# A Strassen pair of the output projection behind both plain column groups

## The chip, the cores and the metric

The kernel runs on one core of one Trainium2 chip. The metric is the device time of one launch in microseconds (us), the median of several runs. All times of the profile are microseconds from the start of the profiled execution's span.

## The reference

One encoder layer: a norm, one input projection, two attention mixers of eight heads each, a gate, one output projection, a norm and the residual. Only the end matters here:

```python
y = jnp.einsum('blc,cd->bld', jnp.concatenate([ya, yb], axis=-1), w_out[layer])
h = h + rmsnorm(y, post_norm_g[layer])
return h[:, N_META:, :]
```

There are 512 real tokens, 2048 mixer channels (16 heads of 128) and 2048 output columns. `rmsnorm` scales a token's row by the inverse root of the mean square over all 2048 columns, so no output row can be finished before all its columns are there.

## The kernel before, in words

**Engines.** TensorE (PE) multiplies; its weight loads are listed as PEld. ScalarE (ACT) and VectorE (DVE) prepare operands and take results, GpSimd (POOL) does some elementwise work and issues the loads of one DMA queue, SyncE (SP) issues those of another. Each engine runs its instructions in the order in which they stand, so a waiting instruction holds up all behind it.

**Precision.** Every product is made of three: each operand is split into a high half (`wh`, `oh`; an ACT copy, L154 and L306) and a low half (`wl`, `ol`; a DVE subtraction, L155 and L309), and the three products without low times low are added up.

**Weights.** `w_out` comes in chunks of 128 x 1024 (512 KB). `todo` (L708) is the list of chunks in the order in which they are used; `fetch` (L194) hands out the next and keeps two more on the way: load on SP to `st`, split to `wh` and `wl`. Each of these tags has three buffers, so a split waits until PE is done with the chunk three before.

**The output projection.** The 2048 columns are four groups of 512, the 512 tokens four tiles of 128. Groups 0 and 3 are plain (`dense_out`, L767): 16 heads x 4 token tiles x 3 matmuls, 192 in all, with one chunk for two heads. Groups 1 and 2 are the middle pair, done by a Strassen scheme: token halves, head halves and the two groups make 2 x 2 blocks, and seven products (`product`, L860) stand for eight. Each product has four chunks of two heads and 48 matmuls. Three products use heads as they are (`of_y`), four use sums of heads:

- `first_sums` (L825) reads, for one of four head pairs, three half tiles `ts` back from DRAM scratch (`oscr`) on POOL's queue and makes from them the operands of the first two of these products (`u`, `v`), split into high and low: four DVE operations and two of ACT for each pair.
- `third_sum` (L834) and `fourth_sum` (L839) make the operands of the other two in the same buffers `u` and `v`, from loads on SP's queue.
- The weights of these four products and of one plain block product are sums of blocks of `w_out` held in `chain[0..3]` (shown as `ch`): two blocks are added while loading, by an accumulating DMA on POOL's queue; the later terms are added by DVE in `summed` (L691), one 128x1024 addition for each chunk, and one block is loaded afresh on the way (L696).

`C(r, x, u)` (L883) is where the results of the middle pair come together, in the output rows `y`: row tile 2x + u, column group 1 + r.

**Order before.** Plain group 0, the seven products, plain group 3. All four pairs' first sums are written out ahead of the first product, all third sums ahead of the fourth, all fourth sums ahead of the fifth; a scheduler then places the instructions on each engine. The last three chunks of group 3 are held together, so that each token tile ends alone and its row is finished (`finish`, L932) while PE works on the next: square sum (ACT), row scale `ry` (POOL), scaling and residual (DVE), store.

**Pools.** The buffers of this stage (`yp`) lie where the attention's lay and become free as attention ends. `pd` and `pd2` are the accumulator pools, four banks each.

## Time and profile before

| | us |
|---|---|
| runs, median (lowest to highest) | 965.67 (964.97 to 966.62) |
| the profiled execution, its own time | 966.93 |
| its span | 965.2 |
| PE busy in the span | 930.0 (96%) |
| DVE busy | 581.5 (60%) |
| ACT busy | 481.7 (50%) |
| POOL busy | 162.9 (17%) |
| last matmul of plain group 0 ends | 812.15 |
| last matmul of the program ends | 955.95 |

The page gives averages over a program whose stages have different limits: PE is busy 96% of the span, so the place to look is where it isn't. A row of the timeline reads: start, duration, engine, line, operation, output<-inputs, shapes, how many instructions are merged, and in brackets the idle time of the engine before it and what ended it. A row of the waits reads: who waited, for whom, the sum in us, how often, the longest.

### The profile page before, as it was taken

What the parts mean: (1) busy time and instruction counts of PE and PEld (TensorE: products, weight loads), DVE (VectorE), ACT (ScalarE), POOL (GpSimd) and SP (SyncE); (2) the same over time, 40 slices, a digit from 0 to 9 for tenths busy, and PEclk for the clock granted to TensorE, in tenths of its full rate; (3) what the DMA queues carried; (4) which work ended last, traced back from release to release, by engine and by line L of the source; (5) the groups of instructions that cost most, each with busy time, mean ns of one, the idle gap of its engine ahead of it and who ended that gap; (6) DMA issues with size and microseconds to landing.
All of it is one profiled execution on the core that took longest, in us unless ns stands there. A gap on an engine that the chain in (4) does not pass through costs nothing.

```text
span 965.2 us, 14195 instructions
## 1 busy us (share of the span) xinstructions
PE 930.0 (96%) x5498; PEld 812.2 (84%) x5498; DVE 581.5 (60%) x974; ACT 481.7 (50%) x844; POOL 162.9 (17%) x255
## 2 busy tenths in 40 slices
PE   9999999999999999999999999989999999796996
PEld 8899898989989898999997888877888888574884
DVE  6375676657476665748653183457555744698626
ACT  6664655546374554637552353354564734452421
POOL 0001010101010010101210042144122213210601
PEclk9999999999999999999999999999999999898998
DMA  9742122222322222222222232212122629976724
GB/s 331 259 157 93 66 87 87 88 87 77 98 77 93 70 99 76 79 86 78 87 78 88 88 91 84 73 59 65 56 77 77 190 95 307 277 224 227 266 82 175
DMA packets 39811, 117.16 MB, mean 121 GB/s; under 512 B 4640, under 2 KB 9632, under 8 KB 39616
## 3 DMA queue, kind: packets, MB, share of 16 engines
q1 hardware_dynamic: 36208, 104.71, 32.7%
q0 software_dynamic: 3392, 11.54, 4.0%
q8 instruction: 43, 0.70, 0.3%
q14 instruction: 24, 0.20, 0.1%
q10 hardware_dynamic: 144, 0.01, 0.0%
HBM read 107.85 MB, written 8.39 MB: 120 GB/s over the span
## 4 chain that ended last, share of the span: by engine, by line
PE 80%; DVE 7%; DMA 5%; POOL 3%; ACT 3%; issue 2%; SPq 0%; DVEq 0%; POOLq 0%; ACTq 0%
PE pd L63 54%; PE po L63 11%; PE sc L63 6%; PE pv L63 4%; PE tr L66 4%; DMA ts<-oscr 2%; DVE wl L155 2%; DVE qn L578 1%; POOL qn L592 1%; DMA ch<-in_w_o_dram 1%; POOL ssh L241 1%; DMA os<-oscr 1%; DVE ch L701 1%; DMA xs<-in_xT_dram 1%; ACT qn L650 0%
## 5 line engine op out<-in xcount | busy, mean ns | idle before, releaser
L63 PE MATMUL pd<-xh,wh 128*128 128x264 f32 (+1 forms) x992 | 333.2, 336 | 0.0
L63 PE MATMUL pd<-xh,wl 128*128 128x264 f32 (+1 forms) x992 | 325.0, 328 | 0.4 <-DVE wl L155 0.4
L63 PE MATMUL pd<-xl,wh 128*128 128x264 f32 (+1 forms) x992 | 324.8, 327 | 0.1
L154 ACT ACTIVATE wh<-st 128x1024 fp32r<-128x1024 f32 (+2 forms) x135 | 140.2, 1039 | 226.7 <-PE pd L63 91.0
L155 DVE TENSOR_TENSOR wl<-st,wh 128x1024 fp32r<-128x1024 f32 (+2 forms) x135 | 162.6, 1205 | 117.4 <-ACT wh L154 116.1
L63 PEld LDWEIGHTS pd<-xh,wl 128*128 128x128 f32 x992 | 186.6, 188 | 17.9 <-DVE wl L155 0.8
L63 PEld LDWEIGHTS pd<-xh,wh 128*128 128x128 f32 x992 | 187.3, 189 | 12.7 <-ACT wh L154 0.2
L63 PEld LDWEIGHTS pd<-xl,wh 128*128 128x128 f32 x992 | 187.5, 189 | 11.7 <-DVE xl L180 0.4
L63 PE MATMUL po<-wl,oh 128*128 128x512 f32 x176 | 70.5, 401 | 9.0 <-DVE wl L155 9.0
L63 PE MATMUL po<-wh,oh 128*128 128x512 f32 x176 | 71.2, 405 | 0.0
L63 PE MATMUL po<-wh,ol 128*128 128x512 f32 x176 | 70.3, 399 | 0.9 <-DVE ol L309 0.9
L463 ACT ACTIVATE p<-p,mx 128x528 f32<-128x528 f32 x64 | 46.5, 728 | 34.1 <-POOL mx L460 34.0
L453 DVE CUSTOM_DVE_ANT_0 p<-sc,dist 128x528 f32<-128x528 f32 x64 | 44.9, 701 | 24.0 <-PE sc L63 23.5
L309 DVE TENSOR_TENSOR pl<-tr,ph 128x512 fp32r<-128x512 f32 x64 | 43.3, 688 | 16.2 <-ACT ph L306 15.0
L306 ACT ACTIVATE ph<-tr 128x512 fp32r<-128x512 f32 x64 | 37.6, 590 | 30.8 <-PE tr L66 30.6
L63 PE MATMUL pd<-wh,xh 128*128 128x512 f32 x128 | 52.2, 408 | 0.8 <-DVE vf L300 0.8
L66 PE MATMUL tr<-ident,p 128*128 128x128 f32 (+1 forms) x320 | 50.7, 273 | 2.3 <-DVE gA L558 1.5
L63 PE MATMUL pd<-wh,xl 128*128 128x512 f32 x128 | 50.6, 395 | 0.0
L63 PE MATMUL pd<-wl,xh 128*128 128x512 f32 x128 | 50.5, 395 | 0.0
L66 PEld LDWEIGHTS tr<-ident,p 128*128 128x128 f32 (+1 forms) x320 | 37.2, 131 | 14.0 <-DVE gA L558 2.4
L63 PEld LDWEIGHTS po<-wl,oh 128*128 128x128 f32 x176 | 33.4, 190 | 18.2 <-DVE wl L155 10.3
L460 POOL TENSOR_SCALAR mx<-mx 128x2 f32<-128x2 f32 x32 | 12.1, 377 | 196.0 <-DVE mx L453 196.0
(204 smaller groups left out, 1565.3 us busy)
## 6 DMA issues: line engine op xcount, KB each, us to landing
st<-in_w_t_dram SPq DMA_DIRECT2D x82, 512.0 KB, 3.6
st<-in_w_o_dram SPq DMA_DIRECT2D x40, 512.0 KB, 4.2
st<-in_w_q_dram SPq DMA_DIRECT2D x16, 512.0 KB, 3.6
xs<-in_xT_dram SPq DMA_DIRECT2D x16, 264.0 KB, 5.4
xns<-in_xn_dram SPq DMA_DIRECT2D x8, 512.0 KB, 5.2
ch<-in_w_o_dram POOLq DMA_DIRECT2D x8, 512.0 KB, 7.5
xr<-in_xn_dram POOLq DMA_DIRECT2D x16, 256.0 KB, 6.1
os<-oscr SPq DMA_DIRECT2D x6, 512.0 KB, 3.7
```

The lines of the kernel that those rows point to most:

```text
L63: self._add(self.nc.tensor.matmul(out, lhsT, rhs, start=start, stop=stop), us)
L66: self._add(self.nc.tensor.transpose(out, in_, ident), 0.109)
L154: nc.scalar.activation(wh[:, c], st[:, c], AF.Copy)
L155: nc.vector.tensor_tensor(out=wl[:, c], in0=st[:, c], in1=wh[:, c].bitcast(F32), op=ALU.subtract)
L241: nc.gpsimd.tensor_tensor(out=dst, in0=dst, in1=mhalf[:rows, :dst.shape[1]], op=ALU.pow)
L306: nc.scalar.activation(dst, src, AF.Copy)
L309: nc.vector.tensor_tensor(out=dst, in0=src, in1=h.bitcast(F32), op=ALU.subtract)
L453: nc.vector.tensor_tensor_reduce(out=two(p), in0=sc[:, :, :HALF], in1=two(dist[:, w0:w0 + NT]), scale=1.0, scalar=-3.0e38, op0=ALU.add, op ...
L460: nc.gpsimd.tensor_scalar(out=mx, in0=mx, scalar1=-0.125, scalar2=1.0, op0=ALU.mult, op1=ALU.mult)
L463: nc.scalar.activation(p2[m], p2[m], AF.Exp, scale=0.125, bias=mx[:, m:m + 1], accum_out=sm[:, m:m + 1])
L578: nc.vector.scalar_tensor_tensor(out=raw[:, i, :], in0=raw[:, i, :], scalar=ss[:rows, i:i + 1], in1=g[:rows], op0=ALU.mult, op1=ALU.mult)
L592: nc.gpsimd.tensor_tensor(out=x, in0=x, in1=cos, op=ALU.mult)
```

## The change

Plain group 3 moves from behind the seven products to ahead of them, and the products stand last, with the accumulator pools exchanged. Beside the eight chunks of group 3 stand, chunk by chunk, the loads of the four chain tiles and the first sums, one pair to every second chunk. The third sums are written out step by step beside the fourth product, the fourth sums beside the sixth. `ts` has six buffers in place of five. The DVE additions to the chain lose their own priority. Row tiles 2 and 3 are finished while the last product runs. In that product the last three chunks are held together and run row tile by row tile; after each, `end` finishes row tile 0 or 1.

The diff, cut:

```diff
@@ todo
-    todo += whole(0) + plain(0, 0) + plain(0, 1) + summed((0, 0)) + summed((0, 1))
-    todo += summed((1, 0), fresh=(0, 0)) + summed() + plain(1, 1) + whole(3)
+    todo += whole(0) + whole(3) + plain(0, 0) + plain(0, 1) + summed((0, 0)) + summed((0, 1))
+    todo += summed((1, 0), fresh=(0, 0)) + summed() + plain(1, 1)
@@ summed
-                with tc.high_priority(rank[0]):
-                    nc.vector.tensor_tensor(out=chain[i], in0=chain[i], in1=st, op=ALU.add)
+                nc.vector.tensor_tensor(out=chain[i], in0=chain[i], in1=st, op=ALU.add)
@@ dense_out(g, pool, beside=None), after each chunk
+            if beside:
+                beside(j0 // 2)
@@ sums
-        t = yp.tile([P, 2, NP], F32, name="ts", tag="ts", bufs=5)
+        t = yp.tile([P, 2, NP], F32, name="ts", tag="ts", bufs=6)
...
-        nc.gpsimd.dma_start(out=chain[i], in_=block(1, 0, i))
...
-        nc.gpsimd.dma_start(out=chain[i], in_=block(1, 1, i), accum_op=ALU.add)
+    def first_chain(i):
+        nc.gpsimd.dma_start(out=chain[i], in_=block(1, 0, i))
+        nc.gpsimd.dma_start(out=chain[i], in_=block(1, 1, i), accum_op=ALU.add)
@@ product(ops, pool, beside=None, done=None)
+        for i in range(1 if done else 4):
+            ws = fetch()
             for u in range(2):
+                step(u, i, ws)
+            if beside:
+                beside(i)
+        if done:
+            last = [fetch(len(todo)) for _ in range(3)]
+            for u in range(2):
+                for i in range(3):
+                    step(u, 1 + i, last[i])
+                done(u, pss[u])
@@ order
+    def beside(s):
+        if s < 4:
+            first_chain(s)
+        if s % 2:
+            first_sums(s // 2)
+
     for t in range(TT):
         collect(0, t, first[t])
-    for i in range(4):
-        first_sums(i)
-    for u, ps in enumerate(product(of_y(0, 0), pd2)):
+    for t, ps in enumerate(dense_out(3, pd2, beside)):
+        collect(3, t, ps)
+    for u, ps in enumerate(product(of_y(0, 0), pd)):
...
-    for i in range(4):
-        third_sum(i)
-    for u, ps in enumerate(product(of_t(t2), pd)):
+    for u, ps in enumerate(product(of_t(t2), pd2, third_sum)):
...
-    for i in range(4):
-        fourth_sum(i)
-    for u, ps in enumerate(product(of_y(1, 1), pd2)):
+    for u, ps in enumerate(product(of_y(1, 1), pd)):
...
-    for u, ps in enumerate(product(of_t(t3), pd2)):
+    for u, ps in enumerate(product(of_t(t3), pd, fourth_sum)):
...
-    for u, ps in enumerate(product(of_t(t4), pd)):
-        TTv(out=C(1, 0, u), in0=C(1, 0, u), in1=ps, op=SUB)
-        block_done(1, 0, u)
@@ end
+    def row_block(t, r, x, g, far=False):
+        v = y[t][:, g * 512:(g + 1) * 512]
+        if far:
+            nc.scalar.activation(v, v, AF.Copy, scale=r)
+            TTp(out=v, in0=v, in1=x, op=ALU.add)
+        else:
+            nc.vector.scalar_tensor_tensor(out=v, in0=v, scalar=r, in1=x, op0=ALU.mult,
+                                           op1=ALU.add)
+        load(out[t * P:(t + 1) * P, g * 512:(g + 1) * 512], v)
...
+    with tc.high_priority(AHEAD):
+        for t in range(2):
+            r = row_scale(2 + t)
+            for g in range(4):
+                row_block(2 + t, r, xh_[t][g], g)
...
+    def end(u, ps):
+        TTv(out=C(1, 0, u), in0=C(1, 0, u), in1=ps, op=SUB)
+        square(u, 2, C(1, 0, u))
+        TTv(out=C(1, 0, u), in0=C(1, 0, u), in1=gpB[:, 1024:1536], op=ALU.mult)
+        if u == 1:
+            row_block(0, rs[0], xs(0, 1), 1)
+            row_block(0, rs[0], xs(0, 2), 2)
+        rs.append(row_scale(u))
+        row_block(u, rs[u], xs(u, 0), 0, True)
+        for g in ((3,) if u == 0 else (3, 1, 2)):
+            row_block(u, rs[u], xs(u, g), g)
+
+    product(of_t(t4), pd2, done=end)
-    dense_out(3, pd2, 6, finish)
```

Where the instructions stand then, on the engines that the order concerns. First DVE. Before, in the second product: the splits of that product's second, third and fourth chunk stand among the sums of pairs 1 and 2 (L829 and L831 make the sums out of `ts`, L309 their low halves).

```order
L155 TENSOR_TENSOR wl_8375<-st_8372,wh_8374 128x1024
L309 TENSOR_TENSOR ul1_8274<-ts_8265,uh1_8273 128x512
L831 TENSOR_TENSOR ts_8269<-ts_8269,ts_8265 128x512
L155 TENSOR_TENSOR wl_8397<-st_8394,wh_8396 128x1024
L309 TENSOR_TENSOR vl1_8279<-ts_8269,vh1_8278 128x512
L829 TENSOR_TENSOR ts_8282<-ts_8284,ts_8282 128x512
L831 TENSOR_TENSOR ts_8286<-ts_8286,ts_8282 128x512
L155 TENSOR_TENSOR wl_8415<-st_8412,wh_8414 128x1024
```

Now, in plain group 3: the splits of its sixth chunk (`wl_8363`) and seventh (`wl_8411`) with the sums of pairs 2 and 3 (L818, L820) and the first third sum (L829).

```order
L820 TENSOR_TENSOR ts_8472<-ts_8472,ts_8468 128x512
L309 TENSOR_TENSOR ul2_8476<-ts_8468,uh2_8475 128x512
L155 TENSOR_TENSOR wl_8363<-st_8360,wh_8362 128x1024
L309 TENSOR_TENSOR vl2_8481<-ts_8472,vh2_8480 128x512
L818 TENSOR_TENSOR ts_8544<-ts_8546,ts_8544 128x512
L820 TENSOR_TENSOR ts_8548<-ts_8548,ts_8544 128x512
L829 TENSOR_TENSOR ts_8835<-ts_8835,ts_8833 128x512
L309 TENSOR_TENSOR ul3_8552<-ts_8544,uh3_8551 128x512
L309 TENSOR_TENSOR vl3_8557<-ts_8548,vh3_8556 128x512
L155 TENSOR_TENSOR wl_8411<-st_8408,wh_8410 128x1024
```

The sums have moved from between chunks of 12 matmuls to between chunks of 24, and a split still stands behind a sum that waits for a load. Next POOL's DMA issues at the same place; before:

```order
L822 DMA ch2_8218<-in_w_o_dram 128x1024
L822 DMA ch3_8220<-in_w_o_dram 128x1024
L810 DMA ts_8248<-oscr0_78 128x2x256
L810 DMA ts_8250<-oscr0_78 128x2x256
L810 DMA ts_8252<-oscr4_82 128x2x256
L828 DMA ch0_8214<-in_w_o_dram 128x1024
L810 DMA ts_8265<-oscr1_79 128x2x256
L810 DMA ts_8267<-oscr1_79 128x2x256
```

Now (L824 loads a chain tile, L825 adds to it, L801 loads a `ts`):

```order
L825 DMA ch1_8215<-in_w_o_dram 128x1024
L801 DMA ts_8314<-oscr0_78 128x2x256
L801 DMA ts_8316<-oscr4_82 128x2x256
L824 DMA ch2_8216<-in_w_o_dram 128x1024
L824 DMA ch3_8217<-in_w_o_dram 128x1024
L801 DMA ts_8392<-oscr1_79 128x2x256
L825 DMA ch2_8216<-in_w_o_dram 128x1024
L825 DMA ch3_8217<-in_w_o_dram 128x1024
L801 DMA ts_8394<-oscr1_79 128x2x256
L801 DMA ts_8396<-oscr5_83 128x2x256
L801 DMA ts_8468<-oscr2_80 128x2x256
```

The plain chain loads, which stood together ahead of the `ts` loads, now stand in two pairs, and each accumulating load stands close behind the load that it waits for. Last DVE at the end of the program. Before, the last split of plain group 3 stands ahead of all work on output rows:

```order
L155 TENSOR_TENSOR wl_9119<-st_9116,wh_9118 128x1024
L155 TENSOR_TENSOR wl_9149<-st_9146,wh_9148 128x1024
L858 TENSOR_TENSOR y0_8224<-po_8992,gpB_8222 128x512
L947 SCALAR_TENSOR_TENSOR y0_8224<-y0_8224,ry_9173,xr_8952 128x512
L947 SCALAR_TENSOR_TENSOR y0_8224<-y0_8224,ry_9173,xr_8954 128x512
```

Now, at the end of product 6 and in product 7, whose third and fourth chunk are split in `wl_9185` and `wl_9203`:

```order
L922 TENSOR_TENSOR y1_8221<-y1_8221,po_9015 128x512
L923 TENSOR_TENSOR y2_8222<-y0_8220,y2_8222 128x512
L155 TENSOR_TENSOR wl_9185<-st_9182,wh_9184 128x1024
L923 TENSOR_TENSOR y3_8223<-y1_8221,y3_8223 128x512
L939 SCALAR_TENSOR_TENSOR y2_8222<-y2_8222,ry_9158,xr_9134 128x512
L155 TENSOR_TENSOR wl_9203<-st_9200,wh_9202 128x1024
L939 SCALAR_TENSOR_TENSOR y2_8222<-y2_8222,ry_9158,xr_9135 128x512
```

The last split stands behind the first finished block of row tile 2, which needs that row's scale `ry_9158` from POOL.

More of the change, by code (lines that the diff above doesn't have):

```diff
@@ L766, with dense_out @@
             lo(ol[j + i], st[:, i * SEQ:(i + 1) * SEQ], oh[j + i])
-    def dense_out(g, pool, tail=0, done=None):
+    def dense_out(g, pool, beside=None):
         pss = [pool.tile([P, 512], F32, name="po", tag="pd") for _ in range(TT)]
-        def part(t, j, ws):
-            wh, wl = ws
-            tq, c = slice(t * P, (t + 1) * P), slice(j % 2 * 512, (j % 2 + 1) * 512)
-            mm(pss[t], oh[j][:, tq], wh[:, c], start=(j == 0), stop=False)
-            mm(pss[t], ol[j][:, tq], wh[:, c], start=False, stop=False)
-            mm(pss[t], oh[j][:, tq], wl[:, c], start=False, stop=(j == KT - 1))
-        for j0 in range(0, KT - tail, 2):
-            ws = fetch()
+        for j0 in range(0, KT, 2):
+            wh, wl = fetch()
             for j in (j0, j0 + 1):
@@ L785, in dense_out @@
                     lo(ol[j], gA[4 + i], oh[j])
+                c = slice((j - j0) * 512, (j - j0 + 1) * 512)
                 for t in range(TT):
-                    part(t, j, ws)
+                    tq = slice(t * P, (t + 1) * P)
+                    mm(pss[t], oh[j][:, tq], wh[:, c], start=(j == 0), stop=False)
+                    mm(pss[t], ol[j][:, tq], wh[:, c], start=False, stop=False)
+                    mm(pss[t], oh[j][:, tq], wl[:, c], start=False, stop=(j == KT - 1))
                     lanes.poll()
-        last = [fetch(len(todo)) for _ in range(tail // 2)] if tail else []
-        for t in range(TT):
-            for j in range(KT - tail, KT):
-                part(t, j, last[(j - KT + tail) // 2])
-            if done:
-                done(t, pss[t])
+            if beside:
+                beside(j0 // 2)
         return pss
@@ L858, in collect, with product, step @@
         TTv(out=y[t][:, gs], in0=ps, in1=gpB[:, gs], op=ALU.mult)
[L860 removed]
+    def product(ops, pool, beside=None, done=None):
         pss = [pool.tile([P, 512], F32, name="po", tag="pd") for _ in range(2)]
[L863 to L871 removed]
+        def step(u, i, ws):
+            wh, wl = ws
+            for j in range(2):
+                bh, bl = ops(i, j, u)
+                c = slice(j * 512, (j + 1) * 512)
+                mm(pss[u], bh, wh[:, c], start=(i + j == 0), stop=False)
+                mm(pss[u], bl, wh[:, c], start=False, stop=False)
+                mm(pss[u], bh, wl[:, c], start=False, stop=(i + j == 4))
+        for i in range(1 if done else 4):
+            ws = fetch()
+            for u in range(2):
+                step(u, i, ws)
[7 more added lines that the diff above has]
+                done(u, pss[u])
         return pss
```

60 lines of the change are left out of this document (22 added, 38 removed).

## The prediction

> **What bounds the kernel now.** First the page's 40 slices: where is TensorE (PE) not busy? Only near the end, where VectorE (DVE) is fullest.
>
> ```profile
> PE   9999999999999999999999999989999999796996
> DVE  6375676657476665748653183457555744698626
> ```
>
> So the question is one of the output projection alone. The waits view for PE from 740 us on names what it waited for:
>
> ```profile
> PE po L63 <- DVE wl L155: 16.5, 6, 6.9
> ```
>
> Six waits, 16.5 us, all for the low half of a weight chunk (`wl`), which DVE makes. The stretches between the longest waits (columns: us, PE busy, PEld, DVE, ACT, POOL, granted clock, DMA share, GB/s):
>
> ```profile
> 812.15:829.74 17.59, 17.55 (x75) 13.48 (x73) 12.90 (x17) 8.37 (x11) 7.13 (x9) 1.00 0.89 242
> 829.74:836.59 6.85, 0.00 (x0) 0.00 (x1) 2.58 (x4) 1.79 (x3) 0.72 (x1) 0.76 1.04 324
> 836.59:873.36 36.77, 35.80 (x144) 27.84 (x144) 34.92 (x38) 18.71 (x25) 4.42 (x2) 0.95 0.78 249
> 873.36:875.56 2.20, 0.00 (x1) 0.00 (x0) 2.20 (x3) 1.06 (x1) 0.00 (x0) 1.00 1.07 401
> 878.62:881.64 3.02, 0.00 (x1) 0.01 (x1) 3.02 (x6) 1.69 (x2) 0.00 (x0) 0.90 0.94 323
> 881.64:887.12 5.48, 5.48 (x12) 3.79 (x12) 4.09 (x6) 1.19 (x2) 0.86 (x2) 0.50 0.32 99
> 887.12:890.62 3.50, 0.00 (x1) 0.00 (x1) 3.08 (x5) 1.53 (x3) 0.27 (x1) 0.90 0.46 150
> 890.62:955.95 65.33, 65.32 (x274) 52.50 (x274) 34.71 (x46) 18.80 (x30) 19.18 (x26) 0.97 0.46 162
> ```
>
> ```profile
> 856.08 0.50 PE L63 MATMUL po<-wl,vh 128*128 128x512 f32 x1 [0.71 <-DVE wl L155]
> ```
>
> There are two kinds of wait. In the first (6.85 us) DVE itself stands idle, its next `wl` queued behind a sum whose `ts` load has not landed. In the later ones (2.20, 3.02, 3.50, and 0.71 at 856) DVE is busy throughout and simply late. After a wait the clock is low too: 12 matmuls took 5.48 us at 0.50. The DVE timeline:
>
> ```profile
> 824.42 0.68 DVE L309 TENSOR_TENSOR vl<-ts,vh 128x512 fp32r<-128x512 f32 x1
> 833.98 0.69 DVE L829 TENSOR_TENSOR ts<-ts 128x512 f32<-128x512 f32 x1 [8.88 <-DMA ts<-oscr]
> 835.32 1.22 DVE L155 TENSOR_TENSOR wl<-st,wh 128x1024 fp32r<-128x1024 f32 x1
> 839.99 0.68 DVE L309 TENSOR_TENSOR ul<-ts,uh 128x512 fp32r<-128x512 f32 x1
> 840.59 0.68 DVE L831 TENSOR_TENSOR ts<-ts 128x512 f32<-128x512 f32 x1
> 842.93 2.35 DVE L155 TENSOR_TENSOR wl<-ch,wh 128x1024 fp32r<-128x1024 f32 x2
> 845.20 2.35 DVE L701 TENSOR_TENSOR ch<-ch,st 128x1024 f32<-128x1024 f32 x2
> 934.44 1.23 DVE L155 TENSOR_TENSOR wl<-st,wh 128x1024 fp32r<-128x1024 f32 x1 [4.38 <-ACT wh L154]
> 940.04 1.23 DVE L155 TENSOR_TENSOR wl<-st,wh 128x1024 fp32r<-128x1024 f32 x1 [4.38 <-ACT wh L154]
> ```
>
> Back to back a 128x512 operation costs 0.60 us (839.99 to 840.59) and a 128x1024 one 1.14 (842.93 to 845.20 is two). With PE never waiting, a plain group's chunks of 24 matmuls stand 5.60 us apart (934.44 to 940.04): 0.2333 each. A product's chunk has 12 (2.8 us), a product 48 (11.2), a plain group 192 (44.8).
>
> **What there is to win.** From 812.15, when group 0 ends, 7 x 48 + 192 = 528 matmuls remain: 123.2 us at full pace. They take 955.95 - 812.15 = 143.8. The excess, 20.6, is the 16.5 of waits and 4.1 of low clock. The change removes no matmul, so 20.6 is its ceiling, apart from the tail.
>
> **Moving the sums beside plain group 3.** The first wait goes if the sums' loads land in time. The new group gives DVE eight `wl` (9.1 us) in 44.8 us, so the 16 operations of the first sums (9.6 us), and the eight of the later sums that now stand there (4.8), fit easily. What can fail is head of line: the group's seventh `wl` (needed at 812.15 + 6 x 5.6 = 845.7) stands behind pair 3's sums and the first third sum. On POOL three landings lie in series before it: chain loads 2 and 3 (the accumulating loads wait for them), pair 1 (behind those), pair 3 (in pair 1's slots). The nearest rows:
>
> ```profile
> 802.33 1.86 POOL L810 DMA_DIRECT2D ts<-oscr  x2
> 817.56 0.71 POOL L810 DMA_DIRECT2D ts<-oscr  x1 [13.37 <-DVE ts L829]
> 818.26 1.86 POOL L828 DMA_DIRECT2D ch<-in_w_o_dram  x2
> ```
>
> ```profile
> st<-in_w_o_dram SPq DMA_DIRECT2D x21, 512.0 KB, 4.8
> ts<-oscr POOLq DMA_DIRECT2D x12, 256.0 KB, 11.7
> ch<-in_w_o_dram POOLq DMA_DIRECT2D x4, 512.0 KB, 12.2
> ch<-in_w_o_dram SPq DMA_DIRECT2D x4, 512.0 KB, 5.9
> ```
>
> ```profile
> DMA to landing us min/median/max: 2.6/6.5/13.1
> ```
>
> Estimate: POOL, which now has issued ten loads by 804.2, comes to chain loads 2 and 3 at about 805.5. Between the landings lie two accumulating issues (1.9), two of pair 1 (1.4), pair 1's sums (4 x 0.60), three issues of pair 3 (2.2), then five DVE operations and the split itself (3.0 + 1.2): 12.1. With today's 12.2, 11.7 and 11.7 the seventh `wl` is done at 853.2, 7.5 us late; with 6.5 each (the median of all `ts` loads) at 837, 8.6 early. It breaks even at a mean landing of 9.4 us. I take **no wait**: the slow landings come from 812 to 836, where a 512 KB weight chunk goes every 2.8 us (187 GB/s of some 300: 242 and 324 in the stretches). Beside group 3 it is one per 5.6 us (94), which leaves POOL's loads about 206 GB/s where they had 113, so 11.7 becomes about 6.5. Both ends, 0 and 7.5 (9.3 with the clock), stay for the range. SP's queue takes ten `ts` loads among the weight loads, from about the sixth chunk on; a weight chunk is fetched well over 5 us ahead there, so I cost that at nothing; without that lead it would cost one landing, 5 us.
>
> **The products behind it.** From the split of the first chain chunk to that of the last (products 3 to 6) DVE's order holds 28 operations of 128x1024, as before, and 16 of 128x512 where there were 29. That is 31.9 + 9.6 = 41.5 us in place of 49.3; 7.8 us of the 9.4 that PE waited there (0.71 + 2.20 + 3.02 + 3.50) go with the work. Two POOL multiplications run beside it:
>
> ```profile
> 850.19 2.52 POOL L889 TENSOR_TENSOR y<-y,gpB 128x512 f32<-128x512 f32 x1 [14.50 <-issue]
> 853.05 1.90 POOL L889 TENSOR_TENSOR y<-y,gpB 128x512 f32<-128x512 f32 x1 [0.34 <-ACT jko L853]
> 913.72 3.19 POOL L889 TENSOR_TENSOR y<-y,gpB 128x512 f32<-128x512 f32 x2 [1.45 <-ACT jko L853]
> ```
>
> ```profile
> 852.08 1.71 DVE L701 TENSOR_TENSOR ch<-ch,st 128x1024 f32<-128x1024 f32 x1
> 853.71 2.32 DVE L155 TENSOR_TENSOR wl<-ch,wh 128x1024 fp32r<-128x1024 f32 x1
> ```
>
> Beside them two DVE operations of 1.21 took 1.71 and 2.32, so 1.6 us more: 43.1. DVE has for it 4 products less the last chunk and a half-step of lead: three of its operations (3.4 us) are done before product 3 begins, and the last split is due 8.4 us into product 6, so 3.4 + 33.6 + 8.4 = 45.4. It fits by 2.3 us, if no load holds it up; the fresh chain loads (5.9 us) have some 6.5. I charge **1.0**, since little is spare; the ends are 0 and 9.4 - 7.8 = 1.6, or 4.3 if a wait reaches 3 us and the clock falls (12 matmuls: 5.48 in place of 2.80).
>
> The Trainium skill's page "SBUF — State Buffer", section "Who interferes with whom", says that a DVE instruction with two SBUF inputs and a GpSimd instruction that reads SBUF lock each other out for a whole instruction. The rows agree in kind; by the rule each multiplication could cost DVE its full length alone, about 1.6, so 3.2 in place of 1.6, and the charge would be 2.6 in place of 1.0.
>
> The Trainium skill's page "TensorE: Matmul & The Clock Gate", section "What's actually happening", lets the clock fall after an idle window of about 3.4 us. Here a wait of 3.02 was enough, so the row decides; by the rule the 4.3 would be 1.6.
>
> **The last product.** Its fourth chunk is now needed at 2.8 + 1.4 + 1.4 = 5.6 us after product 6 ends, not 8.4, because the last three chunks are run token tile by token tile. Its `wl` stands behind the first output block of row tile 2, which waits for that tile's scale. After product 6: two DVE operations (1.3 with the start), the square 0.8, POOL's multiplication 1.6, the scale 1.0, the block 0.6, the split 1.2, in all some 6.8 with the hand-overs. That is a wait of **1.2** (0 to 3, should the multiplication take 2.52 and stand beside DVE).
>
> **The tail.** Now 965.2 - 955.95 = 9.2 us:
>
> ```profile
> 956.03 0.60 ACT L853 ACTIVATE jko<-po 128x512 f32<-128x512 f32 x1 [3.51 <-PE po L63]
> 956.33 5.56 SPq L139 DMA_DIRECT2D out_dram<-y  x5
> 957.17 0.55 POOL L937 TENSOR_TENSOR ry<-ry,mhalf 128x1 f32<-128x1 f32 x1
> 957.75 0.72 ACT L944 ACTIVATE y<-y,ry 128x512 f32<-128x512 f32 x1 [1.03 <-POOL ry L937]
> 958.55 1.26 POOL L945 TENSOR_TENSOR y<-y,xr 128x512 f32<-128x512 f32 x1 [0.83 <-ACT y L944]
> ```
>
> ```profile
> out_dram<-y SPq DMA_DIRECT2D x6, 512.0 KB, 2.6
> ```
>
> Afterwards: DVE up to 0.4 late with row tile 0's blocks, a subtraction 0.7, square 0.8, scale 1.0, ACT's block 0.8, POOL's addition 1.3, then four stores whose issues (0.33 each) stand behind that addition on SP, 1.4, a landing of 2.6, about 0.8 to the end of the span (965.2 - 961.89 - 2.5), and hand-overs: 10.2. So **+1.0** (-0.5 to +2). Residual rows and output rows of tiles 2 and 3 are loaded and stored beside the last two products, where DMA has room (162 GB/s in the last stretch).
>
> **Sum.** -20.6 + 0 + 1.0 + 1.2 + 1.0 = -17.4. The profiled execution took 966.93 (span 965.2); it becomes 949.5. The median shown is 965.67, 1.3 below it, so the forecast is **948.3**. Its own range, from 0 to 1.6, 0 to 3 and -0.5 to 2: 944.6 to 951.7.
>
> **Rivals.**
> - *The seventh split late by landings.* For it: 11.7 is measured, and POOL still waits in order. Against it: less weight traffic. At 11.7 it costs 9.3: 957.6; halfway 953. Chance 0.17.
> - *DVE stays the bound in products 3 to 6.* For it: 43.1 of 45.4 us. Against it: 7.8 us of its work are gone. It gives 1.6 to 4.3 in place of 1.0, and up to 9.4 + 4.1 if the old waits recur: 949 to 961, most likely 952. Chance 0.14.
> - *Slower: the same three landings in series, longer than now.* The loss must reach 17.4, of which the clock gives 1.8 (144 matmuls at 0.95 after the 6.85 wait), so 15.6 of lateness: 9.4 + 15.6/3 = 14.6 us mean landing decides. The largest measured is 13.1, and the traffic is less; at 16 it would be 970. Chance 0.05.
> - *It comes to nothing* (landings near 14.6, or late splits in both stages): 964 to 967, chance 0.03. That the order is not what the change says can be excluded: the rows of DVE and POOL show it.
>
> **How the numbers follow.** Forecast 0.59, the two faster rivals 0.31, below 944.6 0.02, slower 0.05, no change 0.03. The range takes the forecast's own and most of both rivals: 944.5 to 957. Faster by over 0.2% (about 2 us, what a measurement here tells apart): 0.92; within it 0.03; slower 0.05.
>
> **What would show it.** Right: plain group 3 runs 44.8 us with no PE wait; PE's waits sum to 1 to 4 us; the clock stays 1.00 to the end; one short wait before the last product's fourth chunk; the tail is about 10. Wrong: a DVE idle for `ts<-oscr` ahead of a `wl` beside group 3 (first rival), DVE without a gap and PE waiting in products 3 to 6 (second), or landings of `ts` over 14 us.

## The result, and the profile after

| | before | after |
|---|---|---|
| median, us (lowest to highest, runs) | 965.32 (964.86 to 966.62, 4) | 955.69 (954.42 to 957.89, 4) |
| ratio, 95% interval | | 0.9901 (0.9880 to 0.9922) |
| span of the profiled execution | 965.2 | 953.9 |
| end of group 0 to the last matmul | 146.6 | 130.9 |
| tail: last matmul to the end of the span | 9.2 | 12.9 |

The change makes the kernel 9.6 us faster; the interval of the ratio lies clear of 1. The forecast was 17.4 faster (its 965.67 before was the median of three of these four runs). First the 40 slices of the page of the changed kernel, PE and DVE:

```profile
PE   9999999999999999999999999998999999999983
DVE  6386576757575574757554274447554662476996
```

The hole in PE (7, 9, 6 near the end, before) is gone but for the last two slices, 8 and 3. DVE is now fullest in the two slices ahead of the last (9, 9). The waits of PE from 740 us on (who, for whom, sum, times, longest), and the rows of the three that lie in the products:

```profile
PE po L63 <- ACT wh L154: 3.1, 1, 3.1
PE po L63 <- DVE wl L155: 2.2, 2, 1.1
```

```profile
920.25 0.50 PE L63 MATMUL po<-wl,uh 128*128 128x512 f32 x1 [1.10 <-DVE wl L155]
928.47 0.50 PE L63 MATMUL po<-wl,vh 128*128 128x512 f32 x1 [1.11 <-DVE wl L155]
932.75 0.79 PE L63 MATMUL po<-wh,vh 128*128 128x512 f32 x1 [3.09 <-ACT wh L154]
940.65 0.39 PE L63 MATMUL po<-wl,vh 128*128 128x512 f32 x1
```

Before, six waits made 16.5 us. Now three make 5.3: one in product 6, two in product 7, the longest for the *high* half of the last chunk, so for its load. The same by stretches (us, PE busy, PEld, DVE, ACT, POOL, clock, DMA share, GB/s):

```profile
810.20:855.00 44.80, 44.80 (x193) 36.04 (x192) 26.15 (x35) 15.51 (x26) 7.51 (x10) 1.00 0.85 265
855.00:900.00 45.00, 45.00 (x197) 36.70 (x196) 37.84 (x38) 25.06 (x34) 4.11 (x2) 1.00 0.63 198
920.25:941.05 20.80, 16.55 (x58) 12.04 (x58) 18.13 (x30) 6.34 (x12) 11.93 (x16) 0.84 0.71 257
932.75:941.05 8.30, 8.24 (x24) 5.82 (x24) 7.50 (x10) 1.37 (x5) 4.96 (x5) 0.70 0.55 209
941.05:953.90 12.85, 0.00 (x0) 0.00 (x0) 7.35 (x9) 2.08 (x4) 5.14 (x4) 0.64 0.49 186
```

Plain group 3 (the first of these stretches) runs without a gap. So do the products up to 900. The rest of the loss stands in the last 34 us: waits, the clock at 0.70 for the 24 matmuls behind the 3.09 wait (8.30 us in place of 5.6), and a tail 3.7 us longer.

**How the stretches below are cut.** Group 0 ends 9 matmuls (2.1 us) after the start of its first square; the row for before reads:

```profile
807.30 0.60 ACT L853 ACTIVATE jko<-po 128x512 f32<-128x512 f32 x1 [2.63 <-PE po L63]
```

So it ended at 809.4, not at 812.15: the table ahead of the change and the prediction took a place 12 matmuls into the first product. From the end of group 0 on, 528 matmuls need 123.2 us at full pace, in every kernel. The excess of before was thus 146.55 - 123.2 = 23.4 (16.5 waits, 6.9 clock) and not 20.6.

### The profile page after: what moved, and what is told of

It is laid out like the page before. It is cut to its first block, busy times and chain, and to the rows that moved or that the text cites. A ratio compares the mean times of both kernels' runs of the same rounds, so it can differ in the third digit from the quotient of the medians.

```text
span 953.9 us, 14190 instructions
## 1 busy us (share of the span) xinstructions
PE 926.4 (97%) x5498; PEld 810.8 (85%) x5498; DVE 584.6 (61%) x974; ACT 482.0 (51%) x845; POOL 164.0 (17%) x250
## 4 chain that ended last, share of the span: by engine, by line
PE 84%; DVE 7%; DMA 2%; POOL 2%; ACT 2%; issue 1%; SPq 0%; DVEq 0%; POOLq 0%; ACTq 0%
PE pd L63 54%; PE po L63 14%; PE sc L63 6%; PE pv L63 5%; PE tr L66 5%; DVE wl L155 1%; DVE qn L578 1%; DMA st<-in_w_o_dram 1%; DVE y L939 1%; POOL qn L592 1%; DMA ch<-in_w_o_dram 1%; POOL ssh L241 1%; DMA xns<-in_xn_dram 1%; DMA xs<-in_xT_dram 1%; ACT qn L650 0%
## 5 line engine op out<-in xcount | busy, mean ns | idle before, releaser
L63 PEld LDWEIGHTS pd<-xh,wh 128*128 128x128 f32 x992 | 187.3, 189 | 12.9 <-ACT xh L179 0.2
L309 DVE TENSOR_TENSOR pl<-tr,ph 128x512 fp32r<-128x512 f32 x64 | 43.4, 688 | 16.2 <-ACT ph L306 15.0
L413 POOL TENSOR_SCALAR pm<-pm 32x256 fp32r<-32x256 f32 x32 | 20.1, 627 | 149.7 <-ACT pm L306 145.8
```

The lines of the kernel that those rows point to most:

```text
L63: self._add(self.nc.tensor.matmul(out, lhsT, rhs, start=start, stop=stop), us)
L309: nc.vector.tensor_tensor(out=dst, in0=src, in1=h.bitcast(F32), op=ALU.subtract)
L413: nc.gpsimd.tensor_scalar(out=pm[32:64], in0=pm[0:32].bitcast(F32), scalar1=1.0, scalar2=1.0, op0=ALU.mult, op1=ALU.mult)
```

## The experiments

All twelve runs side by side, each against the kernel before on the same chip. "Matmuls" is the stretch from the end of group 0 to the last matmul (123.2 is its floor), "tail" the rest of the span. Both are from the profiled execution, the ratio is from the medians. The ends of matmuls are modelled, so a stretch is good to about half a us (the last two come out just under the floor). Group 0 ended between 809.2 and 812.8 in these executions, which stands in neither column.

| run | median | ratio (95%) | matmuls | tail |
|---|---|---|---|---|
| changed kernel | 955.69 | 0.9901 (0.9880 to 0.9922) | 130.9 | 12.9 |
| before_no_first_sums | 954.62 | 0.9889 (0.9863 to 0.9916) | 132.9 | 9.3 |
| after_no_first_sums | 951.69 | 0.9838 (0.9821 to 0.9855) | 124.0 | 14.6 |
| five_head_buffers | 960.9 | 0.9941 (0.9921 to 0.9962) | 130.5 | 17.3 |
| fourth_sums_early | 955.05 | 0.9873 (0.9852 to 0.9894) | 129.4 | 13.0 |
| no_residual_loads | 953.47 | 0.9874 (0.9857 to 0.9891) | 129.7 | 12.0 |
| residual_early | 958.34 | 0.9925 (0.9910 to 0.9939) | 133.9 | 11.9 |
| products_on_dve | 953.26 | 0.9867 (0.9851 to 0.9883) | 125.7 | 16.0 |
| last_chunk_free | 952.8 | 0.9852 (0.9836 to 0.9869) | 126.2 | 14.7 |
| four_row_scales | 953.9 | 0.9865 (0.9845 to 0.9886) | 129.7 | 12.2 |
| all_together | 956.35 | 0.9886 (0.9870 to 0.9903) | 123.5 | 21.0 |
| stores_in_order | 950.38 | 0.9824 (0.9799 to 0.9849) | 122.8 | 14.6 |
| stores_in_order_early_sums | 945.83 | 0.9778 (0.9753 to 0.9804) | 123.1 | 11.4 |

Only after_no_first_sums, last_chunk_free and the two versions with the stores in order have intervals clear of the changed kernel's. For the other runs the difference from the changed kernel is an indication, and what is said of them rests on rows of their traces.

### What the first sums cost, in the old place and in the new

**before_no_first_sums** leaves the first sums out of the kernel before: their loads, DVE and ACT operations. Two column tiles of `gpB` stand in for what the fourth sums take from them, and heads for what the two products take:

```diff
-        TTv(out=b0, in0=b1, in1=b0, op=SUB)
-        t1.append(operand("u", i, b0))
-        TTv(out=a1, in0=a1, in1=b0, op=SUB)
-        t2.append(operand("v", i, a1))
+        t2.append([gpB[:, n * 512:(n + 1) * 512].rearrange("p (i q) -> p i q", i=2) for n in range(2)])
...
-product(of_t(t1), pd) / product(of_t(t2), pd)
+product(of_y(0, 1), pd) / product(of_y(1, 1), pd)
```

> The kernel before with the first sums left out (their loads, their 16 DVE and 8 ACT operations; heads stand in as they are). Theory (those sums cost the kernel before its first wait by their loads, and the later ones by filling DVE): the 6.85 us wait goes with the low clock behind it, the waits of products 3 to 6 fall from 9.4 to under 4, and the time falls by 13 to 19 us, to 946 to 953. Rival (the waits come from the chain's loads and additions, and the sums only stand in the same queue): under 7 us.

It is 10.6 us faster than before, less than the theory's 13 to 19 and more than the rival's 7. The waits of PE that are left (timeline):

```profile
817.17 0.50 PE L63 MATMUL po<-wl,oh 128*128 128x512 f32 x1 [1.50 <-DVE wl L155]
826.22 0.80 PE L63 MATMUL po<-wl,oh 128*128 128x512 f32 x1 [5.98 <-DVE wl L155]
```

The four later waits went with the sums' DVE work. The first stayed, for the loads of the *third* sums, which moved up into the gap (the 1.50 ahead of it goes back to the load of `gpB`, for which DVE stood idle until 814.09). So the old order had two troubles: DVE full, and a queue in which a split stands behind loads.

**after_no_first_sums** makes the same edit on the changed kernel.

> Left out, against the changed kernel: the first sums (16 DVE operations, their 12 loads and 8 ACT copies); stand-ins feed the third and fourth products. Theory A (beside plain group 3 these sums are hidden entirely): no change, 955 to 956.5, and the waits of TensorE stay the last product's. Rival B (their loads still cost something, by crowding or by holding back the seventh split of group 3): 1.5 to 3 us faster, 952.5 to 954. The same edit on the kernel before took away 10.6 us.

More came than the second theory expected, 6 us by the ratios (0.9838 against 0.9901), and not by its mechanism. Beside group 3 there was no PE wait to take away. The gain lies in the last 30 us: with the stand-in the fourth sums depend on nothing and DVE makes all four at 831 to 839, where the changed kernel makes two of them in product 6. Those two are bound up with GpSimd:

```profile
914.77 3.74 POOL L896 TENSOR_TENSOR y<-y,gpB 128x512 f32<-128x512 f32 x2 [0.59 <-ACT jko L847]
```

```profile
915.58 3.49 DVE L834 TENSOR_TENSOR ts<-vh,ts 128x512 f32<-128x512 f32 x2
```

Two DVE operations that take 1.28 alone took 3.49 beside two GpSimd multiplications; this is the 1.10 wait at 920. The run was not the clean test that it was meant to be, hence fourth_sums_early below. The same stand-in is in before_no_first_sums, where the third and fourth sums come earlier too, so its 10.6 us aren't the price of the first sums alone either.

**five_head_buffers** undoes one part of the change (`bufs=6` to `bufs=5` for `ts`).

> The changed kernel with five buffers for the heads' sums (ts), as the kernel before had, instead of six. In the changed kernel the sixth and seventh splits of group 3 were done about 1 and 0.5 us before TensorE needed them, behind sums whose loads took 10 to 12 us to land. Theory A (the landings stand in series and the sixth buffer is what keeps group 3 free of waits): one load more waits for a release, TensorE waits 3 to 8 us in group 3, time 958 to 963 (ratio to before 0.992 to 0.998). Rival B (the margin holds, since a release comes before the queue gets there): no wait in group 3, time as the changed kernel, ratio 0.988 to 0.992.

The time fell into the first theory's range, 960.9, and its mechanism did not happen: group 3 has one wait, of 0.30, at its eighth chunk. The matmuls take 130.5, as in the changed kernel. Some 4.4 of the 5 us are in the tail, 17.3; group 0 ending 1.1 later in this execution is most of the rest. With one buffer less, three of the four fourth sums come after 914, among the last splits, and the last sums of the output blocks so much later that ACT's squares of these blocks stand behind its copy of the last chunk, which waits for a load. The multiplications on GpSimd wait for the squares, the row scale for them:

```profile
932.51 1.06 ACT L154 ACTIVATE wh<-st 128x1024 fp32r<-128x1024 f32 x1 [5.78 <-DMA st<-in_w_o_dram]
933.48 0.61 ACT L847 ACTIVATE jko<-y 128x512 f32<-128x512 f32 x1
```

```profile
934.27 2.93 POOL L896 TENSOR_TENSOR y<-y,gpB 128x512 f32<-128x512 f32 x2 [8.72 <-ACT jko L847]
937.19 0.26 POOL L928 TENSOR_SCALAR ry<-ssy,ssp 128x1 f32<-128x1 f32 x1
```

In the changed kernel that row scale starts at 929.55. A number within a forecast range said nothing of its reason here; the row did.

**fourth_sums_early** is the changed kernel with the loads of the last two fourth sums in idle buffers:

```diff
-        a0 = heads_of(4 + i, lo_, nc.sync)
+        if i < 2:
+            a0 = heads_of(4 + i, lo_, nc.sync)
+        else:
+            a0 = op.tile([P, 2, NP], F32, name="ta", tag=f"oh{i}")
+            nc.sync.dma_start(out=a0, in_=oscr[4 + i].rearrange("i p q -> p i q")[:, :, lo_])
```

> The changed kernel with one edit: the loads of the last two fourth sums go to two idle buffers (oh2, oh3) instead of ts, so their four DVE operations (3.49 and 1.28 us at 915.6 and 920.1 in the changed kernel) run beside the first product. Theory A (the end is bound by DVE's work from product 6 on, and the run without first sums was 6 us faster because its fourth sums came early, not because the first sums cost anything beside group 3): the 1.1 us wait at 920 goes, the last product starts 1 to 2 us earlier, and the time is 951 to 953.5, ratio 0.983 to 0.987. Rival B (the first sums' loads and operations beside group 3 were the cost; the fourth sums only fill gaps): at most 1 us faster, ratio 0.989 to 0.991.

0.9873, between the two theories, and not separable from the changed kernel by the intervals. The four operations did leave product 6, but in their place another operation met the GpSimd pair, and behind it the last chunk's load was late as before:

```profile
915.43 3.48 DVE L309 TENSOR_TENSOR vl<-ta,vh 128x512 fp32r<-128x512 f32 x2
```

```profile
930.61 1.06 ACT L154 ACTIVATE wh<-st 128x1024 fp32r<-128x1024 f32 x1 [5.06 <-DMA st<-in_w_o_dram]
```

So the sums alone are not what bounds the end. How much of the 6 us of after_no_first_sums belongs to which of its effects (sums early, GpSimd's two multiplications apart, the last load issued at 920.51 in place of 922.69) stays open. Early fourth sums gave 2.7 us by the ratios, so up to some 3.4 could still be what the first sums cost in their new place, though PE shows no wait for them there.

### The last product

**no_residual_loads** leaves the residual loads out; `gpB` stands in for the residual rows.

```diff
-            nc.gpsimd.dma_start(out=xl_[t][n], in_=xn[...])
+    xh_ = [[gpB[:, g * 512:(g + 1) * 512] for g in range(4)] for t in range(2)]
+    xs = lambda t, g: gpB[:, g * 512:(g + 1) * 512]
```

> The changed kernel with its 12 residual loads (4 MB) left out; the gain tile stands in for the residual, so the output lacks it. Theory A (these loads crowd the last weight chunk's load, which took 8.85 us to land and cost PE 3.09 us and a low clock): the landing falls below 6 us, the 3.09 wait to 1.7 or less, the clock stays 1.00 in the last product, and the time falls by 3 to 5 us, to about 951 to 953. Rival B (the load lands late because SP issues it late, 922.69): landing and wait stay, time within 1 us of 955.7. Rival C (the split stands behind the first finished row block on DVE and would be late anyway): the landing falls, but a wait of 2 us or more stays, now for DVE, and the time falls by less than 2.5 us.

The load wait of 3.09 is gone: the last chunk lands in 3.6 us. In its place stands a wait of 3.81 for `wl`, by the mechanism of the prediction: the last split behind the first row block, which waits for the row scale:

```profile
931.97 0.69 PE L63 MATMUL po<-wl,vh 128*128 128x512 f32 x1 [3.81 <-DVE wl L155]
```

```profile
928.96 0.75 DVE L939 SCALAR_TENSOR_TENSOR y<-y,ry,gpB 128x512 f32<-128x512 f32 x1 [0.82 <-POOL ry L930]
929.63 2.28 DVE L155 TENSOR_TENSOR wl<-st,wh 128x1024 fp32r<-128x1024 f32 x1
```

The split itself took 2.28 in place of 1.22; a GpSimd multiplication of 1.80, from 929.03, lay beside it. Two causes lie one over the other. Taking away the one that ends last brings 2.2 us by the medians, and the matmuls end only 1.2 sooner, as rival C expected.

**residual_early** moves the residual loads to buffers that are free from product 2 on (`oh`, `ol`), issued ahead of product 3.

```diff
+    xr = [[op.tile([P, 512], F32, name="xr", tag=f"o{'hl'[t // 2]}{t % 2 * 4 + g}") for g in range(4)]
+          for t in range(TT)]
```

> The changed kernel with the 16 residual tiles in the buffers of heads 0 to 7, free since product 1, and their loads issued on POOL from there on. If the crowding of the last product's loads is what costs (theory A): as without the loads, 951 to 953, unless 4 MB more beside products 2 to 5 make PE wait there, of which the fresh chain loads (4.4 us landing) would be the first sign. If they only move the crowding (rival): PE waits 2 us or more in products 3 to 6 and the time stays at 955 to 957.

By the medians 2.7 us slower than the changed kernel. The crowding moved along: the loads were now issued from 859 to 875, a weight chunk issued there, at 861.74, took 8.76 us (the median of before was 4.8), PE waits three times between 871 and 891, and at the end the row block makes its wait again:

```profile
871.71 0.50 PE L63 MATMUL po<-wh,oh 128*128 128x512 f32 x1 [0.81 <-ACT wh L154]
938.75 0.50 PE L63 MATMUL po<-wl,vh 128*128 128x512 f32 x1 [3.80 <-DVE wl L155]
```

In both places the loads cost something beside the weight chunks; and without the late chunk at the end (its load no longer bounds), the second cover alone holds PE up for 3.80.

**products_on_dve** moves the multiplications of finished blocks from GpSimd to DVE.

```diff
-        TTp(out=C(r, x, u), in0=C(r, x, u), in1=gpB[:, g * 512:(g + 1) * 512], op=ALU.mult)
+        TTv(out=C(r, x, u), in0=C(r, x, u), in1=gpB[:, g * 512:(g + 1) * 512], op=ALU.mult)
```

> The changed kernel with the six multiplications by the gain, 128x512 each, that POOL does on the middle pair's blocks done by DVE. Theory (POOL and DVE hold each other up, so that the two in product 6 cost DVE 2.2 us and PE the wait of 1.10 at 920): two DVE operations that took 3.49 us take 1.28, the wait at 920 goes although DVE has 3.6 us more to do, and time falls by 1 to 2 us. Rival (DVE is simply full there): PE waits longer in products 3 to 6, 2 us or more in all, and the time rises by 1 to 3 us.

Six operations *more* on the fullest engine, and the matmuls end 5.2 us sooner. The two in product 6:

```profile
912.92 1.29 DVE L896 TENSOR_TENSOR y<-y,gpB 128x512 f32<-128x512 f32 x2
```

They cost 1.3 on DVE, where from GpSimd they had cost DVE 2.2 of standstill. That alone is not 5.2. In the changed kernel the standstill (the DVE pair runs from 915.58 to 919.07) also delays the split of the last product's first chunk (921.45), and with it the load of the fourth (922.69), which the next run takes up. Here that split starts at 917.07, in part because one of the fourth sums now stands behind it, and the load at 918.31. The wait of 3.09 is gone with the 1.10; waits of 1.02 and 0.52 stand there instead. Of the 5.2 the tail takes back 3.1 (16.0): ten row blocks start on DVE at PE's end or later, where seven did.

**last_chunk_free** gives the last chunk's load the idle buffer `ch0` (residual rows go elsewhere), and puts its split ahead of all row blocks.

```diff
+    def final():
+        st = yp.tile([P, 1024], F32, name="stl", tag="ch0")
+        nc.sync.dma_start(out=st, in_=block(1, 1, 3))
+        return wsplit(st)
-    todo += ... + plain(1, 1)
+    todo += ... + plain(1, 1)[:3] + [final]
...
             last = [fetch(len(todo)) for _ in range(3)]
+            rows_far()
```

> The changed kernel with two edits for the fourth chunk of the last product: its load goes to the idle buffer ch0 and no longer waits for the first chunk's slot, and its low half is split ahead of all row blocks. Theory A (two covers, one behind the other, make the 4.2 us of waits and some 2.7 us of low clock there: the late load, and behind it the row block, which gave 3.8 us without the residual loads): both waits go, TensorE ends 4 to 6 us earlier, and the time is 950 to 952.5. Rival B (the row blocks only move into the tail, and DVE with GpSimd sets the end): TensorE ends earlier but the tail grows by as much, 954 to 956. Rival C (crowding by the residual loads alone made the load late): the wait stays at 2 us or more.

Both covers are off: the longest wait is 1.17, all three sum to 3.3, and the clock stays up.

```profile
PE po L63 <- DVE wl L155: 3.3, 3, 1.2
921.00:938.00 17.00, 14.04 (x58) 10.65 (x58) 16.26 (x27) 5.86 (x10) 10.85 (x14) 1.00 0.69 232
```

Matmuls 126.2, 4.7 less. The tail takes 1.8 of it back, and the time, 952.8, lies just above the first theory's range. This is how the 3.09 came about: with three `st` buffers the fourth chunk's load waits until the first chunk is split (921.5 to 922.7 in the changed kernel), and then lands beside nine of the twelve residual loads:

```profile
922.69 8.85 DMA st<-in_w_o_dram
```

### The tail

**four_row_scales** gives `ry` four buffers in place of two. In the changed kernel the last row scale stood behind a row block that still read its buffer.

```diff
-        r = yp.tile([P, 1], F32, name="ry", tag="ry", bufs=2)
+        r = yp.tile([P, 1], F32, name="ry", tag="ry", bufs=4)
```

> The changed kernel with four buffers instead of two for the row scale ry. Theory A (the last row scale waits for a DVE row block that still reads the buffer, in the tail): the 0.75 us wait of GpSimd goes and the row scale meets fewer DVE operations, tail 12.85 to about 12.0, time 954.5 to 955.3. Rival B (it waits for the square all the same, and the DVE sets the tail): no change, 955.3 to 956.

The tail is 0.7 shorter in the profiled execution. The ratio is 0.9865 (0.9845 to 0.9886); its interval overlaps that of the changed kernel slightly, so it points to a small gain and does not prove it. The matmul stretch is 1.1 shorter too, and the 1.10 wait of product 6 is absent, though DVE's order there is the same: single executions differ by as much.

**all_together**: products on DVE, the last chunk freed, four row scales, and no row block on GpSimd.

> The changed kernel with the multiplications of finished blocks on DVE, the fourth chunk's load in a buffer of its own, its split ahead of the row blocks, four row scales, and all row blocks on DVE. Theory A (these are separate losses: 3.8 us of waits, 1.5 us more at the last chunk with its clock, about 1 to 3 us of tail): 945 to 949. Rival B (all lie on one DVE, whose work merely moves into the tail): 951 to 953.5, no better than with the products on DVE alone.

PE is nearly at its floor, 123.5, and the kernel is no faster than the changed one, slower than either theory said, for the tail is 21.0. Windows of the tail (last column GB/s):

```profile
939.00:944.00 5.00, 0.00 (x0) 0.00 (x0) 4.56 (x8) 0.00 (x0) 1.29 (x2) 0.50 0.13 48
944.90:953.00 8.10, 0.00 (x0) 0.00 (x0) 0.90 (x2) 0.00 (x0) 0.00 (x0) 0.50 1.00 379
```

DVE worked while hardly a store ran, and then 12 stores ran at the full rate with DVE nearly done. The stores stand on SP's queue in the order of the row tiles 2, 3, 0, 1; DVE had come to make tile 3's blocks last. Eight finished blocks stood behind four unfinished ones.

**stores_in_order** has the same edits with the row blocks of tiles 2 and 3 ahead on DVE, and the last subtractions early (the scheduler again places the last split and the row blocks itself):

```diff
-    with tc.high_priority(AHEAD):
+    with tc.high_priority(0):
         for t in range(2):
             r = row_scale(2 + t)
...
+        with tc.high_priority(200):
             TTv(out=C(1, 0, u), in0=C(1, 0, u), in1=ps, op=SUB)
             square(u, 2, C(1, 0, u))
+            rs.append(row_scale(u))
```

> As the run with all edits together (products on DVE, the fourth chunk's load in a buffer of its own, four row scales, all row blocks on DVE), but the row blocks of tiles 2 and 3 come on DVE ahead of those of tiles 0 and 1, in the order of the stores on SyncE's queue, and the subtraction of the last row tile ahead of most of them. In the run with all edits TensorE ended 7.5 us earlier than in the changed kernel, but 12 of the 16 stores were issued after 943.8, behind those of tile 3, whose blocks DVE made last, and needed 8 us at 380 GB/s. Theory A (the order of stores against blocks ate the gain): the stores run beside the blocks, the tail is 12 to 14 us, span 946 to 948, time 948 to 950, ratio 0.981 to 0.984. Rival B (the work of DVE behind the last product sets the end, whatever the order): tail 16 us or more, time 951.5 to 954, ratio 0.985 to 0.988.

6 us faster by the order of the same work (0.9824 against 0.9886); what the early subtractions give of it is not separated. Its tail is 14.6, and DVE has no gap in it until its last row block:

```profile
937.37 7.37 DVE L944 SCALAR_TENSOR_TENSOR y<-y,ry,xr 128x512 f32<-128x512 f32 x11
```

**stores_in_order_early_sums** adds the edit of fourth_sums_early.

> The run with the stores in order and this edit: the four operations of the last two fourth sums (2.4 us) run beside the first product. Theory A (DVE, without a gap from product 6 to its last row block, sets the end): 2 to 2.5 us faster than the run with the stores in order, ratio 0.979 to 0.981. Rival B (the stores set the end: 380 GB/s from 940 on): less than 1 us faster, ratio 0.9815 to 0.983.

945.83, ratio 0.9778 (0.9753 to 0.9804), more than was expected, and the best of all: by the medians 4.5 us faster than stores_in_order for 2.4 us less DVE work at the end (the intervals overlap slightly, the runs themselves don't). The matmuls were at their floor already; the tail fell from 14.6 to 11.4, since the first row block starts at 928.57 in place of 932.83: the small operations of the row scale no longer stand behind the sums. PE now runs to its end without a break beside a DVE that is busy all the time:

```profile
920.00:933.70 13.70, 13.70 (x61) 11.02 (x59) 13.70 (x27) 5.28 (x9) 7.26 (x9) 1.00 0.70 249
933.70:945.10 11.40, 0.00 (x0) 0.00 (x0) 7.95 (x13) 0.72 (x2) 3.78 (x4) 0.68 0.71 268
```

The edit that was worth nothing sure on the changed kernel is worth 4.5 here, since here DVE's work is what the end waits for. This version, 21.6 us below the kernel before by the medians, beats both kernels of this study.

## Why the prediction was right, and where it was not

Direction, range (944.5 to 957.0) and main mechanism held: with the first sums' work beside group 3 all six waits of before are gone, and that work shows no wait of PE in its new place. The forecast of 948.3 was 7.4 too low, and that the range held was in part luck: the forecast's own part of it ended at 951.7, the rest was there for two rivals (a late split in group 3, DVE as the bound in products 3 to 6), and neither of them is what made the time longer. By the spans, -11.3 in place of -17.4:

| term | forecast | measured |
|---|---|---|
| excess of before (a ceiling) | -20.6 | -23.4 |
| plain group 3 | 0 | 0 |
| products 3 to 7: waits | 1.0 + 1.2 | 1.1 + 4.2 |
| the same: low clock | 0 | 2.3 |
| tail | +1.0 | +3.7 |
| group 0 ends later, in this execution | - | +0.8 |

- **"From 812.15, when group 0 ends"** was a misread row. It made the ceiling too small by 2.8, which by itself would have pushed the forecast further down, to 945.5. One error hid another.
- **"I take no wait" for group 3** was right, and its reason was not. The prediction let the landings of `ts` on POOL's queue fall from 11.7 to 6.5 us, since the weight traffic halves. From 800 to 860 their median was 12.0, with DMA 0.85 busy in group 3; only the three of pair 3, the last of the series (issued from 831.10 on), took 4.0:

```profile
ts<-oscr POOLq DMA_DIRECT2D x11, 256.0 KB, 12.0
ts<-oscr POOLq DMA_DIRECT2D x3, 256.0 KB, 4.0
```

  A split stood behind a sum whose load had not landed, as the first rival said:

```profile
830.12 0.69 DVE L818 TENSOR_TENSOR ts<-ts 128x512 f32<-128x512 f32 x1 [6.66 <-DMA ts<-oscr]
842.04 1.22 DVE L155 TENSOR_TENSOR wl<-st,wh 128x1024 fp32r<-128x1024 f32 x1
```

  The seventh split was done at 843.26 and needed at 810.2 + 6 x 5.6 = 843.8. The rival missed by half a us, because the third landing of the series was short and POOL issued the chain loads at 803.4, two us earlier than estimated. It was worth more than its 0.17.
- **Products 3 to 6, 1.0**: the size was right (one wait of 1.10, in product 6). What made it is what the prediction priced for the two multiplications at 913.72: a DVE pair stretched to 3.49. The page "SBUF — State Buffer" of the Trainium skill, section "Who interferes with whom", has a DVE instruction with two SBUF inputs and a GpSimd instruction that reads SBUF shut each other out; the trace agrees, with 3.49 for 1.28 beside 3.74 on GpSimd.
- **"The last product", 1.2, failed**: it measured 4.2, and 2.3 of low clock. The mechanism that was priced, the split behind the row block, is real but larger than priced (3.81 in no_residual_loads), and lay under a later one. The prediction took the load of the fourth chunk for granted. It is bound to the first chunk's split by the three buffers, that split stands behind the stretched DVE pair of product 6, and the load took 8.85 us among the residual loads, which the prediction had put where "DMA has room". last_chunk_free removes both and gives 4.7 us of matmul time.
- **The tail, 1.0, was mis-sized**: 3.7. The prediction summed the last row tile's chain with 0.4 us for a busy DVE and none for GpSimd. DVE still had row blocks of other tiles: the last subtraction began at 942.30, 1.25 after PE, and the last row scale took 1.12 in place of 0.27:

```profile
942.30 0.68 DVE L968 TENSOR_TENSOR y<-y,po 128x512 f32<-128x512 f32 x1
942.89 1.82 DVE L939 SCALAR_TENSOR_TENSOR y<-y,ry,xr 128x512 f32<-128x512 f32 x2
946.04 3.08 DVE L939 SCALAR_TENSOR_TENSOR y<-y,ry,xr 128x512 f32<-128x512 f32 x3 [0.71 <-POOL ry L930]
```

```profile
944.25 1.12 POOL L928 TENSOR_SCALAR ry<-ssy,ssp 128x1 f32<-128x1 f32 x1 [0.75 <-DVE y L939]
```

- **The deeper fault** is that the prediction treated the last product and the tail as two terms. Before, the last group left DVE little to do. Now sums, splits, blocks and row tiles meet there, and much of what PE gains by an earlier end, DVE owes afterwards: products_on_dve shortens the matmuls by 5.2 us and is 3.3 faster by the ratios (0.9901 - 0.9867, of 966). In all_together, 7.4 shorter and only 1.4 faster, the order of the stores took most of it back. In stores_in_order, with both out of the way, DVE's row blocks run on without a gap behind PE's end: the bound moved from DVE beside PE to DVE behind PE.

## What to carry to other kernels

When work moves to the end of a program, add up everything that the busiest side engine has to do from there to the last store, and not the waits of the main engine alone. A load into a rotating buffer is as early as the release of that buffer; look up which instruction frees it before calling the load hidden. Keep the order of stores in one queue the order in which their data is made, and when an experiment lands in the forecast range, look at the rows before believing the reason.

## What the runs showed of the hardware that had not been expected

- Six multiplications moved from GpSimd onto the fullest engine made the kernel faster. Two of 128x512 take DVE 1.29; beside them on GpSimd (3.74) two DVE operations took 3.49 in place of 1.28. The price isn't fixed: in residual_early GpSimd's two took 7.83, and the first DVE pair beside them stayed at 1.29.
- Tiny GpSimd operations suffer as well: the 128x1 row scale took 0.27 with DVE idle and 1.12 to 1.73 beside row blocks, and it stands on the chain that ends the kernel. Before the change it took 0.27 (956.82) beside a DVE operation too, one of 0.69 from 956.76 that reads one input from the accumulators.
- Stores of 256 KB ran at 379 GB/s with the DMA engines at 1.00. Sixteen of them need 11 us at that rate, more than the whole tail of before (9.2), so the output of all four row tiles can't wait for the last matmul.
- Loads on GpSimd's queue landed in a median of 12.0 us beside plain group 3, though weight chunks came half as often as in the products; ten loads of the same size and source on SyncE's queue took 4.0 in the same stretch. Those came later, though, and the three on GpSimd's queue from 831.10 on took 4.0 as well, so the queue alone is not shown to be the cause.
- After the wait of 3.09 us the clock was 0.70 over the next 8.3 us; after those of 1.1 the second matmul was at 0.39 us again. But the clock fell 1.24 us into that wait, and in products_on_dve it was at 0.50 for 3.4 us right behind waits of 1.02 and 0.52:

```profile
929.66:930.90 1.24, 0.01 (x1) 0.00 (x0) 0.45 (x1) 0.00 (x0) 1.16 (x2) 1.00 0.90 354
930.90:932.75 1.85, 0.00 (x0) 0.00 (x0) 0.77 (x2) 1.11 (x2) 0.00 (x0) 0.50 0.35 141
928.71:932.12 3.41, 3.41 (x9) 2.63 (x10) 2.99 (x13) 1.45 (x4) 0.85 (x3) 0.50 0.00 0
```

  (The first two lines are of the changed kernel.) In last_chunk_free, waits of 1.02, 1.13 and 1.17 left it at 1.00. So the length of one wait doesn't decide, and no run here shows what does. The Trainium skill's page "TensorE: Matmul & The Clock Gate", section "What's actually happening", lets the clock fall after an idle window of about 3.4 us. The traces differ: as before the change (3.02), less was enough.
